# A two-layer encoder trunk on one core: tanh for silu beside the heads, scores in single banks, a one-tensor maxima step, and another order of the first fetches

## The chip, the cores and the metric

The kernel runs on one core of a Trainium2 chip. Its engines are TensorE (PE, with its weight loads PEld), VectorE (DVE), ScalarE (ACT), GpSimd (POOL) and SyncE (SP, which here only issues DMAs). They run side by side, each through its own list of instructions in order, and wait for each other by semaphores. The metric is the device time of one execution in microseconds (us), as the median of several runs.

## The reference

Two inputs, `x_sample` (512 tokens) and `x_prompt` (1024 tokens), pass through the same trunk of two layers with a width of 1024. All arithmetic is float32.

```python
def fourier_mixer(x, g, w):                       # layer 0
    h = rms_norm(x, g).reshape(b, s, 8, 128)
    return jnp.real(jnp.fft.fft2(h, axes=(1, 3), norm="ortho")).reshape(b, s, d) @ w

def attention_mixer(...):                         # layer 1: 8 query heads, 2 key heads of 128
    q, k, v = split(rms_norm(x, g) @ w_qkv)
    q, k = apply_rope(rms_norm(q)), apply_rope(rms_norm(k))
    p = softmax(q @ k.T * 128 ** -0.5)            # per head, float32
    return (p @ v) @ w_o

def swiglu_ffn(x, g, w_gate, w_up, w_down):       # after each mixer, inner width 2816
    h = rms_norm(x, g)
    return (jax.nn.silu(h @ w_gate) * (h @ w_up)) @ w_down

for i in range(2):
    x = x + (fourier_mixer if i == 0 else attention_mixer)(x, ...)
    x = x + swiglu_ffn(x, ...)
```

## The kernel before

Tokens are worked in three blocks of 512 (`TB`): block 0 is sample, blocks 1 and 2 are prompt. Activations lie transposed, 128 features by 512 tokens a tile. Each float32 product is three PE passes over operands that are split into a high part (a cast on ACT) and a low rest (a subtraction on DVE or POOL): `split` writes both (lines 242 and 243), `mm3` issues the three matmuls (lines 249 to 251). So every weight chunk costs a load, an ACT cast and a POOL subtraction before PE can use it.

The stages in order of time: the **front** (mixer of sample, with the Fourier transform as matmuls), sample's first SwiGLU woven with prompt's mixer, prompt's first SwiGLU (both blocks together, by a scheme with seven products for eight), then from about 1300 us the **heads**: sample's attention, and prompt's attention woven with sample's second SwiGLU; at the end prompt's second SwiGLU. Two generators are woven by `weave`: stage "F" is the main one, stage "X" the one beside it. Each `yield` gives an estimated cost, and the generator that is behind runs next. A scheduler then sets the final order of each engine's list; instructions through `pinned` keep the order in which they were written.

The front. `turned_weights` prepares the mixer's weight in eight pieces. `load(n)` fetches piece n (line 637, queue of SP), `operand(n)` forms the sum of its halves on DVE (line 648) and the difference on POOL (line 649), casts on ACT (line 651) and subtracts on POOL (line 652); `product(n)` multiplies it on PE (g, with line 667 for an odd row, and c at line 669) and stores it for prompt. `lead` weaves it with `mixer("s", ...)`, which needs sample's rows (`load_rows`, line 404, four pieces on the queues of SP and ACT), their squares, the reciprocal root `r_s`, and the transform matrix `mat_s` (line 1453, POOL's queue). `busy(36)` is a run of matmuls on ones ahead of the first real one. `mixer_projection` multiplies the two results.

The heads. In `attend`, `scores(qc)` makes the scores of 128 queries: for prompt against 1024 keys in one tile of two PSUM banks (`bank2`, one buffer), for sample against 512 keys in one bank (`bankg`). Then come the maxima on DVE (line 1371, one per bank), their maximum times the negative gain (line 1372, the *maxima step*), the exponential on ACT with its row sum (line 1375), the reciprocal on DVE (line 1376) and the scaling on ACT (line 1377). `turned` transposes the result on PE (line 1389) and splits it; `values` multiplies by v. `side` and `sides` give spare banks to other helpers of the same stage.

Sample's second SwiGLU is `ffn(1, 0, ...)`, where `here` is false: 22 chunks of the gate go through silu (line 852) on ACT, which stands in the same list as the exponentials:

```python
dve.tensor_tensor(ga, ga, first["r"], op=ALU.mult)
act.activation(s, ga, AF.Silu)
pool.tensor_tensor(s, s, first["r"], op=ALU.mult)
dve.tensor_tensor(up, up, s, op=ALU.mult)
```

Of the kernel before, what the change touches and what calls it, by code (L numbers as in the profile page):

```python
# [17 lines left out]
P = 128  # L18
# [107 lines left out]
def trunk_kernel(ctx: ExitStack, tc: tile.TileContext, t: dict):  # L126
# [18 lines left out]
    for name, kw in (("sbH", {}), ("sbF", {}), ("sbX", {}), ("psF", PS), ("psX", PS)):  # L145
# [5 lines left out]
    BUFS = {  # L151
# [4 lines left out]
    }  # L156
    uid = [0]
# [37 lines left out]
    def bankg():  # L195
        return tl("g", [TB], F32, "gF", pools["psF"])

    def side():

        return bankg() if cur[0] == "F" else bank2()[:, 0]  # L200

    def sides():
        if cur[0] == "F":
            return [bankg(), bankg()]
        a2 = bank2()
        return [a2[:, 0], a2[:, 1]]

# [45 lines left out]
    early = []  # L253
    nxt, first = {}, {}

    def pinned(ins):
# [373 lines left out]
    def turned_weights(w64, dd, odd, alt):  # L630


        raws = []

        def load(n):
            raw = tl("raw", [2, TB], F32, "rawX")
            sp.dma_start(raw.rearrange("p k n -> p (k n)"), t["wf"][n])
            raws.append(raw)

        load(0)  # L640
        load(1)
        yield
        ods, ready = [], []

        def operand(n):
            raw = raws.pop(0)
            f = tl("f", [2, TB], F32, "rawF")
            pinned(dve.tensor_tensor(f[:, 0], raw[:, 0], raw[:, 1], op=ALU.add))
            pool.tensor_tensor(f[:, 1], raw[:, 0], raw[:, 1], op=ALU.subtract)
            w = moving_w[n % 4]  # L650
            pinned(act.copy(w[:, 0], f))
            pool.tensor_tensor(w[:, 1], f, w[:, 0].bitcast(F32), op=ALU.subtract)
            if n + 2 < NC:
                load(n + 2)
            ready.append(w)

        def product(n):
            h, j = divmod(n, 4)
            if j == 0:
                ods.append(tl("c", [TB], F32, "cX", pools["psX"]))  # L660
            od, w = ods[h], ready.pop(0)
            wt = tl("w", [2, 2, TB], F32R, "wX" if h else "wF")
            for k in range(2):
                ps = bankg()
                mm3(ps, dd[:, 2 * k], dd[:, 2 * k + 1], w[:, 0, k], w[:, 1, k], True, k == 1)
                if k == 0:
                    pe.matmul(ps, alt[0:96, j], w64[0:96, h * TB : (h + 1) * TB], start=False, stop=True)
                    for b in range(2):
                        pe.matmul(od[0:96], odd[:, 8 - 2 * j : 104 - 2 * j], w[:, b, 0], start=j == 0 and b == 0, stop=j == 3 and b == 1)
                split(wt[:, 0, k], wt[:, 1, k], ps)  # L670
                c = tl("t", [TB], F32, "tX")
                act.copy(c, ps)
                sp.dma_start(cwd[h][:, :, k, j, :], c.rearrange("p (n c) -> p n c", n=4))
            turned.append(wt)
            if j == 3:
                stacked(odds[0:96, h * TB : (h + 1) * TB], od[0:96], 64)

        for n in range(3):
            operand(n)
            yield  # L680
        for n in range(NC):
# [77 lines left out]
    def ffn(layer, b, h, out=None):  # L759
# [50 lines left out]
        for fc in range(NF):  # L810
# [41 lines left out]
            act.activation(s, ga, AF.Silu)  # L852
            pool.tensor_tensor(s, s, first["r"], op=ALU.mult)
            dve.tensor_tensor(up, up, s, op=ALU.mult)
            m = tl("mid", [2, TB], F32R, "mid")
            split(m[:, 0], m[:, 1], up)
            if odd_:
# [13 lines left out]
    def moving(blocks, gain, out, ring, helped):  # L871
# [23 lines left out]
        for j in range(4):  # L895
            flush()
            x4, v = loaded.pop()
            a2 = bank2()
            for (d, k), x in list(v.items()):
                if d == k:  # L900
                    v[d, k] = a2[:, d]
# [423 lines left out]
    def attend(blocks, straight, slot):  # L1325
# [6 lines left out]
        for g in range(NKV):  # L1332
# [24 lines left out]
            for h in range(g * GROUP, (g + 1) * GROUP):  # L1357
# [2 lines left out]

                def scores(qc):
                    qs = slice(qc * P, (qc + 1) * P)
                    sc = bankg().unsqueeze(1) if nb == 1 else bank2()
                    for kb in range(nb):
                        ks = slice(kb * TB, (kb + 1) * TB)
                        mm3(sc[:, kb], qt[:, 0, qs], qt[:, 1, qs], kt[:, 0, ks], kt[:, 1, ks], True, True)
                    s_in = sc[:, 0:nb].rearrange("p b n -> p (b n)")
                    gq = 4 * blocks[0] + qc
                    st = col(3)
                    for kb in range(nb):  # L1370
                        dve.tensor_reduce(st[:, 2 * kb : 2 * kb + 1], sc[:, kb], op=ALU.max, axis=AX.X)  # L1371
                    dve.scalar_tensor_tensor(st[:, 1:2], st[:, 2 * nb - 2 : 2 * nb - 1], st[:, 0:1], nrqc[:, gq, h : h + 1], op0=ALU.max, op1=ALU.mult)  # L1372
                    sm = col(2)
                    p = tmp(T) if nb == 1 else tl("p", [T], F32, "pX", ap)
                    act.activation(p, s_in, AF.Exp, bias=st[:, 1:2], scale=rqc[:, gq, h : h + 1], accum_out=sm[:, 0:1])  # L1375
                    dve.reciprocal(sm[:, 1:2], sm[:, 0:1])
                    act.activation(p, p, AF.Copy, scale=sm[:, 1:2])
                    return p
# [63 lines left out]
    got_s, got_p = {}, {}  # L1442

    def row_in(seq):
        m = mpt.tile([P, 2, 258], F32R, tag="rowm", name=f"rowm_{seq}")
        pool.dma_start(m[0:1].rearrange("p h n -> p (h n)"), t[f"row_{seq}"])
        rows_m[seq] = m
# [7 lines left out]
    row_in("s")  # L1455
# [19 lines left out]
    ws = turned_weights(w64, dd, odd, alt)  # L1475

    def lead():
        next(ws)
        sp.dma_start(stage[0:96], t["wf64"])
        m = mixer("s", got_s, u_s, xrs_s, zz_s)  # L1480
        for k, v in enumerate(m):
            yield v
            if k == 3:
                stacked(w64[0:96], stage[0:96], 64)
            if k < 3 or k % 2 == 0 and k < 14:
                next(ws)

    def follow():
        m = mixer_projection("s", got_s)
        for k in range(3):  # L1490
            next(m)
            next(ws)
            yield 1.0
        for _ in ws:
            yield 1.0
# [30 lines left out]
    def aux_0():  # L1526
        load_rows("p")
        row_in("p")
        m_p = [acc_tile("mat_p", [2, 1028], F32R) for _ in range(2)]
        for c in range(2):  # L1530
            pool.dma_start(m_p[c].rearrange("p h n -> p (h n)"), t["dft_p"][:, 2056 * c : 2056 * (c + 1)])
# [177 lines left out]
```

## Time and profile before

| | us |
|---|---|
| median of 3 runs (2921.27 to 2924.79) | 2921.47 |
| the profiled execution: time | 2916.32 |
| the profiled execution: span | 2914.5 |
| PE busy | 2834.5 (97%) |
| ACT table loads, 26 of 1.283 us | 33.4 |

The span runs from the first to the last instruction. A busy PE is not PE at its peak, since matmuls are pipelined and a lowered clock makes them longer; the granted clock was 0.996 on average. In the groups, `out<-in` are tile names without buffer numbers, `x96` is a count, then follow the busy time and the mean in ns of one, and behind the bar the idle time of the engine before them and what ended it.

### The profile page before, as it was taken

What the parts mean: (1) busy time and instruction counts of PE and PEld (TensorE: products, weight loads), DVE (VectorE), ACT (ScalarE), POOL (GpSimd) and SP (SyncE); (2) the same over time, 40 slices, a digit from 0 to 9 for tenths busy, and PEclk for the clock granted to TensorE, in tenths of its full rate; (3) what the DMA queues carried; (4) which work ended last, traced back from release to release, by engine and by line L of the source; (5) the groups of instructions that cost most, each with busy time, mean ns of one, the idle gap of its engine ahead of it and who ended that gap; (6) DMA issues with size and microseconds to landing.
All of it is one profiled execution on the core that took longest, in us unless ns stands there. A gap on an engine that the chain in (4) does not pass through costs nothing.

```text
span 2914.5 us, 37209 instructions
## 1 busy us (share of the span) xinstructions
PE 2834.5 (97%) x13656; PEld 2341.5 (80%) x13656; DVE 1714.5 (59%) x3023; ACT 1304.7 (45%) x2134; POOL 1573.4 (54%) x976
## 2 busy tenths in 40 slices
PE   7999999999999999999999999999999999999999
PEld 6778878888888887787778888888888788888887
DVE  6664562466666666847656565553345466666666
ACT  6543242333333333646757776763333333333332
POOL 4445375767776676432332123224637667766774
PEclk9999999999999999999999999999999999999999
DMA  7435474766556653732332112115448865566553
GB/s 233 143 113 179 139 285 174 287 210 227 195 178 215 219 188 112 238 93 92 94 102 84 34 63 71 55 55 184 159 151 303 326 237 195 179 215 221 195 174 116
DMA packets 178870, 490.53 MB, mean 168 GB/s; under 512 B 19488, under 2 KB 29728, under 8 KB 177280
## 3 DMA queue, kind: packets, MB, share of 16 engines
q1 hardware_dynamic: 177760, 483.36, 48.7%
q0 software_dynamic: 640, 3.74, 0.4%
q8 instruction: 108, 1.77, 0.3%
q10 hardware_dynamic: 288, 1.05, 0.1%
q14 instruction: 74, 0.61, 0.1%
HBM read 422.01 MB, written 66.06 MB: 167 GB/s over the span
## 4 chain that ended last, share of the span: by engine, by line
PE 44%; DVE 3%; issue 2%; ACT 1%; DMA 1%; POOL 1%; SPq 0%; POOLq 0%; DVEq 0%; ACTq 0%
PE a L249 6%; PE a L251 6%; PE a L250 6%; PE c L249 5%; PE c L250 5%; PE c L251 5%; PE g L251 3%; PE g L249 3%; PE g L250 3%; PE c L1389 2%; DVE col L1372 1%; DVE col L1371 1%; DVE acc L1074 1%; POOL w L288 0%; ACT p L1375 0%
## 5 line engine op out<-in xcount | busy, mean ns | idle before, releaser
L288 POOL TENSOR_TENSOR w<-raw,w 128x1024 fp32r<-128x1024 f32 x200 | 479.6, 2404 | 762.3 <-ACT w L287 713.8
L243 POOL TENSOR_TENSOR w<-raw,w 128x512 fp32r<-128x512 f32 (+1 forms) x464 | 608.7, 1332 | 443.6 <-ACT w L242 431.6
L242 ACT CAST w<-raw 128x512 fp32r<-128x512 f32 (+1 forms) x464 | 279.5, 632 | 541.1 <-PE a L251 179.7
L287 ACT CAST w<-raw 128x1024 fp32r<-128x1024 f32 x200 | 209.4, 1049 | 275.2 <-PE g L251 94.5
L249 PE MATMUL g<-h,w 128*128 128x512 f32 x704 | 279.0, 396 | 3.5 <-DVE ss L339 2.0
L249 PE MATMUL a<-ring,w 128*128 128x512 f32 x708 | 277.4, 392 | 0.0
L251 PE MATMUL g<-h,w 128*128 128x512 f32 x704 | 276.2, 392 | 0.0
L250 PE MATMUL g<-h,w 128*128 128x512 f32 x704 | 276.1, 392 | 0.0
L251 PE MATMUL a<-ring,w 128*128 128x512 f32 x708 | 275.9, 390 | 0.0
L250 PE MATMUL a<-ring,w 128*128 128x512 f32 x708 | 275.7, 389 | 0.0
L1074 DVE TENSOR_TENSOR acc<-g,acc 128x512 f32<-128x512 f32 x294 | 201.8, 687 | 105.1 <-PE g L251 104.9
L1074 DVE TENSOR_TENSOR acc<-c,acc 128x512 f32<-128x512 f32 x294 | 201.7, 686 | 92.8 <-PE c L251 91.2
L249 PE MATMUL c<-mid,w 128*128 128x512 f32 x604 | 237.0, 392 | 7.0 <-DVE acc L780 4.9
L250 PE MATMUL c<-mid,w 128*128 128x512 f32 x604 | 236.4, 391 | 4.8 <-DVE mid L243 4.8
L251 PE MATMUL c<-mid,w 128*128 128x512 f32 x604 | 236.1, 391 | 0.0
L249 PE MATMUL c<-h,w 128*128 128x512 f32 x480 | 190.5, 398 | 2.1 <-ACT h L245 1.6
L250 PE MATMUL c<-h,w 128*128 128x512 f32 x480 | 188.7, 395 | 0.4 <-DVE h L246 0.2
L251 PE MATMUL c<-h,w 128*128 128x512 f32 x480 | 188.2, 393 | 0.0
L780 DVE TENSOR_TENSOR acc<-c,acc 128x512 f32<-128x512 f32 x176 | 121.0, 688 | 112.7 <-PE c L251 111.8
L249 PEld LDWEIGHTS a<-ring,w 128*128 128x128 f32 x708 | 133.0, 188 | 32.1 <-DVE mid L243 4.3
L249 PEld LDWEIGHTS g<-h,w 128*128 128x128 f32 x704 | 132.5, 188 | 30.1 <-DVE ss L339 2.2
L251 PEld LDWEIGHTS a<-ring,w 128*128 128x128 f32 x708 | 133.1, 188 | 27.9
(393 smaller groups left out, 6727.5 us busy)
## 6 DMA issues: line engine op xcount, KB each, us to landing
ring<-mov_B SPq DMA_DIRECT2D x248, 512.0 KB, 5.5
ring<-mov_T SPq DMA_DIRECT2D x88, 512.0 KB, 5.2
raw<-in_gate_dram SPq DMA_DIRECT2D x44, 512.0 KB, 3.6
raw<-in_up_dram SPq DMA_DIRECT2D x44, 512.0 KB, 3.5
raw<-in_down_dram SPq DMA_DIRECT2D x88, 256.0 KB, 3.0
raw<-in_gate_dram SPq DMA_DIRECT2D x88, 256.0 KB, 5.1
raw<-in_up_dram SPq DMA_DIRECT2D x88, 256.0 KB, 5.3
raw<-in_down_dram SPq DMA_DIRECT2D x44, 512.0 KB, 4.3
```

Of the source, the lines that this page charges most:

```text
L242: keep(act.copy(hi, src))
L243: keep(eng.tensor_tensor(lo, src, hi.bitcast(F32), op=ALU.subtract))
L249: pe.matmul(out, lh, rh, start=first, stop=False, **kw)
L250: pe.matmul(out, lh, rl, start=False, stop=False, **kw)
L251: pe.matmul(out, ll, rh, start=False, stop=last, **kw)
L287: pinned(act.copy(flat[:, 0], raw)) if early else act.copy(flat[:, 0], raw)
L288: pool.tensor_tensor(flat[:, 1], raw, flat[:, 0].bitcast(F32), op=ALU.subtract)
L780: dve.tensor_tensor(acc[dc], box[0], acc[dc], op=ALU.add)
L1074: dve.tensor_tensor(acc, chain[d], acc, op=ALU.add)
L1371: dve.tensor_reduce(st[:, 2 * kb : 2 * kb + 1], sc[:, kb], op=ALU.max, axis=AX.X)
L1372: dve.scalar_tensor_tensor(st[:, 1:2], st[:, 2 * nb - 2 : 2 * nb - 1], st[:, 0:1], nrqc[:, gq, h : h + 1], op0=ALU.max, op1=ALU.mult)
L1389: pe.transpose(tr[:, i * P : (i + 1) * P], p[:, kc * P : (kc + 1) * P], ident)
```

## The change

Four edits. In `ffn`, where `here` is false, silu(x) is computed as 0.5 x (1 + tanh(x/2)): a tanh on ACT, a new SCALAR_TENSOR_TENSOR on DVE, and the factor 0.5 in the last product. In the heads, once `apart` is set (just before prompt's attention), scores lie in two tiles of one bank each instead of one tile of two, with two buffers of that kind; the exponential is issued once per bank, and a small sum joins the two row sums. `side`, `sides` and `moving` take single banks from then on. The maxima step is a `tensor_scalar` with two per-partition scalars. In the front, piece 0 of the weight is fetched ahead of sample's rows, and `mask`, `mat_s` and the short row `rowm_s` are issued later, inside `lead`.

```diff
+    def single():
+        return tl("a", [TB], F32, "gH", pools["psX"])
     def side():
-        return bankg() if cur[0] == "F" else bank2()[:, 0]
+        return bankg() if cur[0] == "F" else single() if apart else bank2()[:, 0]
...
         load(0)
+        yield
         load(1)
         yield
...
-            act.activation(s, ga, AF.Silu)
+            if here:
+                act.activation(s, ga, AF.Silu)
+            else:
+                act.activation(s, ga, AF.Tanh, scale=0.5)
+                dve.scalar_tensor_tensor(s, s, 1.0, ga, op0=ALU.add, op1=ALU.mult)
             pool.tensor_tensor(s, s, first["r"], op=ALU.mult)
-            dve.tensor_tensor(up, up, s, op=ALU.mult)
+            if here:
+                dve.tensor_tensor(up, up, s, op=ALU.mult)
+            else:
+                dve.scalar_tensor_tensor(up, up, 0.5, s, op0=ALU.mult, op1=ALU.mult)
...
-                    sc = bankg().unsqueeze(1) if nb == 1 else bank2()
+                    sc = [bankg()] if nb == 1 else sides()
...
-                    dve.scalar_tensor_tensor(st[:, 1:2], st[:, 2 * nb - 2 : 2 * nb - 1], st[:, 0:1], nrqc[:, gq, h : h + 1], op0=ALU.max, op1=ALU.mult)
-                    sm = col(2)
+                    dve.tensor_scalar(st[:, 1:2], st[:, 2 * nb - 2 : 2 * nb - 1], st[:, 0:1], nrqc[:, gq, h : h + 1], op0=ALU.max, op1=ALU.mult)
+                    sm = col(3)
                     p = tmp(T) if nb == 1 else tl("p", [T], F32, "pX", ap)
-                    act.activation(p, s_in, AF.Exp, bias=st[:, 1:2], scale=rqc[:, gq, h : h + 1], accum_out=sm[:, 0:1])
+                    for kb in range(nb):
+                        act.activation(p[:, kb * TB : (kb + 1) * TB], sc[kb], AF.Exp, bias=st[:, 1:2], scale=rqc[:, gq, h : h + 1], accum_out=sm[:, 2 * kb : 2 * kb + 1])
+                    if nb == 2:
+                        dve.tensor_scalar(sm[:, 0:1], sm[:, 0:1], sm[:, 2:3], None, op0=ALU.add)
...
-    load_rows("s")
     m_s = acc_tile("mat_s", [2, 2, 514], F32R)
-    pool.dma_start(m_s.rearrange("p c h n -> p (c h n)"), t["dft_s"])
...
-    sp.dma_start(mask, t["mask"])
+    ws = turned_weights(w64, dd, odd, alt)
+    next(ws)
+    load_rows("s")
     zz_s = zeros("s")
...
     def lead():
         next(ws)
+        sp.dma_start(mask, t["mask"])
+        next(ws)
+        pool.dma_start(m_s.rearrange("p c h n -> p (c h n)"), t["dft_s"])
         sp.dma_start(stage[0:96], t["wf64"])
+        row_in("s")
+        rows_of_dft("s")
```

What the scheduler makes of it. In the front, POOL's list before began with the matrix `mat_s`, the short row and the constants (`eo`), and then came the first differences of the weight's pieces:

```order
L1453 DMA mat_s_162<-in_dft_s_dram 128x2056
masks.py:199 ISA
masks.py:199 AFFINE_SELECT ident<-ident 128x128
L1446 DMA rowm_s<-in_row_s_dram 1x12x43
L1460 DMA eo_166<-in_dft_d_dram 128x1136
L443 MEMSET t_172 128x480
L649 TENSOR_TENSOR f_266<-raw_239 128x512
L649 TENSOR_TENSOR f_283<-raw_241 128x512
L652 TENSOR_TENSOR wm_169<-f_266,wm_169 128x1024
```

The same place now (line numbers are those of the changed kernel, tile numbers differ):

```order
L1473 DMA eo_157<-in_dft_d_dram 128x1136
masks.py:199 ISA
masks.py:199 AFFINE_SELECT ident<-ident 128x128
L448 MEMSET t_170 128x480
L655 TENSOR_TENSOR f_240<-raw_162 128x512
L1494 DMA mat_s_156<-in_dft_s_dram 128x2056
L1463 DMA rowm_s<-in_row_s_dram 1x12x43
L655 TENSOR_TENSOR f_273<-raw_237 128x512
L658 TENSOR_TENSOR wm_160<-f_240,wm_160 128x1024
```

The constants come first, and the matrix and the short row are issued between the first two differences. PE's list in the front before, from the second half of piece 0 (g_345) on, where c_402 and c_414 are the mixer's:

```order
L251 MATMUL g_345<-wm_169,eo_166 128x512
L669 MATMUL c_331<-wm_169,eo_166 96x512 x4
L249 MATMUL c_402<-mat_s_162,comb_238 128x258
L250 MATMUL c_402<-mat_s_162,comb_238 128x258
L249 MATMUL c_414<-mat_s_162,comb_238 128x258
```

And now, from the same place to the first matmul that reads the matrix:

```order
L256 MATMUL g_327<-wm_160,eo_157 128x512
L675 MATMUL c_313<-wm_160,eo_157 96x512 x2
L673 MATMUL g_315<-eo_157 128x512
L675 MATMUL c_313<-wm_160,eo_157 96x512
L254 MATMUL g_362<-wm_160,eo_157 128x512
...
L673 MATMUL g_403<-eo_157 128x512
L254 MATMUL g_415<-wm_160,eo_157 128x512
L255 MATMUL g_415<-wm_160,eo_157 128x512
L256 MATMUL g_415<-wm_160,eo_157 128x512
L254 MATMUL c_431<-mat_s_156,comb_236 128x258
```

The products of pieces 0, 1 and 2 (g_315 to g_415) now stand ahead of the mixer. In the heads, DVE's list before, around the maxima step of one chunk of prompt's attention (pt is the split transposed result of the chunk before):

```order
L1371 TENSOR_REDUCE col_13746<-a_13739 128x1 x2
L243 TENSOR_TENSOR pt_13761<-c_13763,pt_13761 128x4x128
L1372 SCALAR_TENSOR_TENSOR col_13746<-col_13746,nrqc 128x1
L243 TENSOR_TENSOR pt_13762<-c_13770,pt_13762 128x4x128
L1376 RECIPROCAL col_13750<-col_13750 128x1
```

And now, with the tanh's new step (L862) between the maxima of two banks:

```order
L1383 TENSOR_REDUCE col_13870<-a_13862 128x1
L862 SCALAR_TENSOR_TENSOR t_13977<-t_13977,g_13712 128x512
L1383 TENSOR_REDUCE col_13870<-a_13863 128x1
L1384 TENSOR_SCALAR col_13870<-col_13870,nrqc 128x1
L1390 TENSOR_SCALAR col_13874<-col_13874 128x1
L1391 RECIPROCAL col_13874<-col_13874 128x1
```

The small sum L1390 is new and stands ahead of the reciprocal. ACT's list at a silu before:

```order
L852 ACT_TABLE_LOAD
L852 ACTIVATE t_14313<-g_13922 128x512
L242 CAST pt_14039<-c_14085 128x4x128
L242 CAST pt_14040<-c_14092 128x4x128
L1375 ACT_TABLE_LOAD
L1375 ACTIVATE p_14081,col_14080<-a_14069,col_14076,rqc 128x1024
```

And now at a tanh (L861), between the halves of a chunk's exponential and its scaling (L1392):

```order
L1388 ACTIVATE p_13599,col_13598<-a_13586,col_13594,rqc 128x512
L1388 ACTIVATE p_13599,col_13598<-a_13587,col_13594,rqc 128x512
L247 CAST pt_13560<-c_13612 128x4x128
L861 ACTIVATE t_13688<-g_13318 128x512
L1392 ACTIVATE p_13599<-p_13599,col_13598 128x1024
```

No table load stands there any more; the whole list has 4 where it had 26.

More of the change, by code (lines that the diff above doesn't have):

```diff
@@ L204, in sides @@
             return [bankg(), bankg()]
+        if apart:
+            return [single(), single()]
         a2 = bank2()
@@ L251, in mm3 @@
         pe.matmul(out, ll, rh, start=False, stop=last, **kw)
-    early = []
+    early, apart = [], []
     nxt, first = {}, {}
@@ L897, in moving @@
             x4, v = loaded.pop()
-            a2 = bank2()
+            a2 = sides()
             for (d, k), x in list(v.items()):
                 if d == k:
-                    v[d, k] = a2[:, d]
+                    v[d, k] = a2[d]
                 dve.scalar_tensor_tensor(v[d, k], x, gain[:, 4 * d + j : 4 * d + j + 1], r[k], op0=ALU.mult, op1=ALU.mult)
@@ L1362, in scores @@
                     qs = slice(qc * P, (qc + 1) * P)
-                    sc = bankg().unsqueeze(1) if nb == 1 else bank2()
+                    sc = [bankg()] if nb == 1 else sides()
                     for kb in range(nb):
                         ks = slice(kb * TB, (kb + 1) * TB)
-                        mm3(sc[:, kb], qt[:, 0, qs], qt[:, 1, qs], kt[:, 0, ks], kt[:, 1, ks], True, True)
-                    s_in = sc[:, 0:nb].rearrange("p b n -> p (b n)")
+                        mm3(sc[kb], qt[:, 0, qs], qt[:, 1, qs], kt[:, 0, ks], kt[:, 1, ks], True, True)
                     gq = 4 * blocks[0] + qc
@@ L1370, in scores @@
                     for kb in range(nb):
-                        dve.tensor_reduce(st[:, 2 * kb : 2 * kb + 1], sc[:, kb], op=ALU.max, axis=AX.X)
-                    dve.scalar_tensor_tensor(st[:, 1:2], st[:, 2 * nb - 2 : 2 * nb - 1], st[:, 0:1], nrqc[:, gq, h : h + 1], op0=ALU.max, op1=ALU.mult)
-                    sm = col(2)
+                        dve.tensor_reduce(st[:, 2 * kb : 2 * kb + 1], sc[kb], op=ALU.max, axis=AX.X)
+                    dve.tensor_scalar(st[:, 1:2], st[:, 2 * nb - 2 : 2 * nb - 1], st[:, 0:1], nrqc[:, gq, h : h + 1], op0=ALU.max, op1=ALU.mult)
+                    sm = col(3)
                     p = tmp(T) if nb == 1 else tl("p", [T], F32, "pX", ap)
-                    act.activation(p, s_in, AF.Exp, bias=st[:, 1:2], scale=rqc[:, gq, h : h + 1], accum_out=sm[:, 0:1])
+                    for kb in range(nb):
+                        act.activation(p[:, kb * TB : (kb + 1) * TB], sc[kb], AF.Exp, bias=st[:, 1:2], scale=rqc[:, gq, h : h + 1], accum_out=sm[:, 2 * kb : 2 * kb + 1])
+                    if nb == 2:
+                        dve.tensor_scalar(sm[:, 0:1], sm[:, 0:1], sm[:, 2:3], None, op0=ALU.add)
                     dve.reciprocal(sm[:, 1:2], sm[:, 0:1])
@@ L1444, in row_in, with rows_of_dft @@
     def row_in(seq):
-        m = mpt.tile([P, 2, 258], F32R, tag="rowm", name=f"rowm_{seq}")
-        pool.dma_start(m[0:1].rearrange("p h n -> p (h n)"), t[f"row_{seq}"])
-        rows_m[seq] = m
+        rows_m[seq] = mpt.tile([P, 2, 258], F32R, tag="rowm", name=f"rowm_{seq}")
+    def rows_of_dft(seq):
+        pool.dma_start(rows_m[seq][0:1].rearrange("p h n -> p (h n)"), t[f"row_{seq}"])
     turned = []
     odds = mpt.tile([P, D], F32R, name="odds")
-    load_rows("s")
     m_s = acc_tile("mat_s", [2, 2, 514], F32R)
-    pool.dma_start(m_s.rearrange("p c h n -> p (c h n)"), t["dft_s"])
     mats["s"] = [m_s[:, 0], m_s[:, 1]]
-    row_in("s")
     slot = h_slot("eo", F32R, "B")
@@ L1482, in lead @@
             yield v
-            if k == 3:
+            if k == 1:
                 stacked(w64[0:96], stage[0:96], 64)
-            if k < 3 or k % 2 == 0 and k < 14:
+            if k < 2 or k % 2 == 0 and k < 14:
                 next(ws)
@@ L1491, in follow @@
             next(m)
-            next(ws)
+            next(ws, None)
             yield 1.0
@@ L1528, in aux_0 @@
         row_in("p")
+        rows_of_dft("p")
         m_p = [acc_tile("mat_p", [2, 1028], F32R) for _ in range(2)]
@@ L1609, in trunk_kernel @@
     open_pool("psX", **RIGHT, **PS)
+    apart.append(True)
     ap = open_pool("ap", **RIGHT)
```

1 line of the change is left out of this document (removed), and 2 rows, old and new, of the table BUFS.

## The prediction

> **What bounds the kernel now.** I read first the page's busy line, then a table of stages, then who waits for whom inside the two stages that the change touches.
>
> ```profile
> PE 2834.5 (97%) x13656; PEld 2341.5 (80%) x13656; DVE 1714.5 (59%) x3023; ACT 1304.7 (45%) x2134; POOL 1573.4 (54%) x976
> core 0: us, PE busy (x) PEld busy (x) DVE busy (x) ACT busy (x) POOL busy (x), PEclk, DMA share, GB/s
> 0.00:20.00 20.00, 14.80 (x89) 13.60 (x89) 9.47 (x17) 10.12 (x19) 7.73 (x13) 1.00 0.82 287
> 20.00:30.00 10.00, 3.70 (x10) 1.74 (x10) 9.35 (x23) 4.61 (x7) 7.54 (x5) 0.83 0.36 111
> 30.00:40.00 10.00, 6.37 (x18) 4.69 (x19) 7.62 (x11) 6.02 (x12) 3.21 (x3) 0.50 0.62 208
> 40.00:100.00 60.00, 53.69 (x346) 46.69 (x345) 44.27 (x101) 38.70 (x69) 25.65 (x16) 1.00 0.64 196
> 100.00:1300.00 1200.00, 1183.82 (x5491) 973.88 (x5490) 713.91 (x1231) 462.65 (x769) 725.67 (x451) 1.00 0.56 191
> 1300.00:2000.00 700.00, 669.58 (x3743) 560.47 (x3742) 414.06 (x839) 470.36 (x730) 203.97 (x97) 1.00 0.24 77
> 2000.00:2300.00 300.00, 294.86 (x1307) 243.21 (x1306) 113.23 (x188) 96.60 (x144) 173.67 (x98) 0.99 0.64 219
> ```
>
> TensorE (PE) bounds the program and no matmul is added or removed, so all that can be won is time in which PE stands still or runs at a lowered clock. PE is idle for 2914.5 - 2834.5 = 80.0 us. Two stages hold most of it: the front (0 to 100 us), 100 - 14.80 - 3.70 - 6.37 - 53.69 = 21.4 us, and the heads (1300 to 2000 us), 700 - 669.58 = 30.4 us. PE works through one list in order, so a gap that closes there moves everything behind it; from 2000 us on PE is nearly full and the saving arrives at the end.
>
> **The heads: what PE waits for.** The view of waits, PE alone, 1300 to 2000 us (total, times, longest), then the maxima step L1372 in the view of one line (min/median/max ns, and who waited), the by-form groups on VectorE (DVE), and one piece of the timeline.
>
> ```profile
> PE a L249 <- ACT p L1375: 7.2, 7, 2.1
> PE c L1389 <- ACT p L1377: 5.0, 5, 1.5
> PE c L1389 <- DVE h L243: 3.4, 4, 1.4
> PE c L1389 <- ACT t L1403: 2.1, 2, 1.3
> PE c L1389 <- ACT t L1377: 1.4, 1, 1.4
> PE g L249 <- ACT t L1375: 1.3, 2, 0.9
> L1372 DVE SCALAR_TENSOR_TENSOR col<-col,nrqc x96: 199/218/2407, 1342.3 to 1976.3; 128x1 f32<-128x1 f32 x96
>   ACT p L1375: 49.2, 35
> L1372 DVE SCALAR_TENSOR_TENSOR col<-col,nrqc 128x1 f32<-128x1 f32 x96 | 59.6, 624 | 1.1
> L1376 DVE RECIPROCAL col<-col 128x1 f32<-128x1 f32 x96 | 15.4, 160 | 51.8 <-ACT p L1375 43.9 <-ACT t L1375 7.5
> 1576.42 2.41 POOL L243 TENSOR_TENSOR w<-raw,w 128x1024 fp32r<-128x1024 f32 x1 [6.37 <-ACT w L242]
> 1576.58 2.27 DVE L1372 SCALAR_TENSOR_TENSOR col<-col,nrqc 128x1 f32<-128x1 f32 x1
> 28.13 2.60 POOL L652 TENSOR_TENSOR wm<-f,wm 128x1024 fp32r<-128x1024 f32 x1
> 28.45 0.13 DVE L437 TENSOR_SCALAR m<-m 128x1 f32<-128x1 f32 x1
> ```
>
> L1372 handles one element a partition, yet its mean is 624 ns against a median of 218. The timeline shows why: it starts 0.16 us after a GpSimd (POOL) instruction and ends with it (1578.85 against 1578.83). It reads two tensors from SBUF. L1376 reads one, is as small, and stays at 160 ns on average over 96 instructions. The exponential (L1375, ScalarE, ACT) waits for L1372 for 49.2 us in all, the scores' bank is free only after the exponential, and PE's transposes (L1389) need its scaled result.
>
> **Part 1, the maxima step with one tensor (96 instructions).** The two maxima and the gain become one tensor and two per-partition scalars of a TENSOR_SCALAR. The nearest row of that form is L437: 0.13 us in the middle of a POOL instruction that runs from 28.13 to 30.73. If the new step behaves so, it costs some 0.2 us, the old median, and 96 x (0.624 - 0.218) = 39 us of blocked DVE time go. What of it lies on PE's path is at most the six waits above, which all stand behind the softmax chain or behind DVE's queue: 7.2 + 5.0 + 3.4 + 2.1 + 1.4 + 1.3 = 20.4 us. A lower bound is 0 (the new form waits as the old). I take 17, because the blockings (up to 2.4 us) are as long as PE's gaps (up to 2.1 us); the rest has other causes.
>
> The Trainium skill, "SBUF — State Buffer", section "Who interferes with whom", says that a VectorE instruction with two SBUF inputs contends with a GpSimd instruction that reads SBUF, and the second to issue waits for the whole of the first; the trace agrees (2.27 us beside 2.41). The same section lists tensor_scalar among the operations that can take both ports and then contend; by that the saving would be 0. The section "What auto-detection actually checks" of the Trainium skill's "VectorE: DVE Perf Modes" speaks of the outermost non-unit dimensions of source and destination for that mode, and a column of one element has none; the 0.13 us of L437 agrees.
>
> **Part 2, silu by tanh in sample's second SwiGLU, and part 3, exponentials by halves.** Table loads, and the shapes that the halves are priced by:
>
> ```profile
> L1375 ACT ACT_TABLE_LOAD x12 | 15.4, 1283 | 0.2
> L852 ACT ACT_TABLE_LOAD x12 | 15.4, 1283 | 0.2
> L1375 ACT ACTIVATE p<-a,col,rqc 128x1024 f32<-128x1024 f32 x64 | 77.4, 1209 | 49.5 <-DVE col L1372 49.2
> L1375 ACT ACTIVATION_READ_ACCUMULATOR p<-a,col,rqc 128x1 f32 x64 | 12.3, 192 | 0.0
> L1375 ACT ACTIVATE t<-g,col,rqc 128x512 f32<-128x512 f32 x32 | 24.9, 779 | 17.2 <-DVE col L1372 17.2
> L1307 DVE SCALAR_TENSOR_TENSOR t<-c,gains,rope 128x512 f32<-128x512 f32 x13 | 9.7, 748 | 11.2 <-ACT a L1306 10.9 <-issue 0.3
> 1619.21 1.28 ACT L852 ACT_TABLE_LOAD   x1
> 1619.24 0.50 PE L249 MATMUL a<-w,w 128*128 128x512 f32 x1 [2.11 <-ACT p L1375]
> ```
>
> In the new program 22 of the table loads are gone: 22 x 1.283 = 28.2 us of ACT. The tanh itself I price as the silu. DVE gets 22 more SCALAR_TENSOR_TENSOR of 128x512 (748 ns by L1307): 16.5 us. The halves turn 64 x (1.209 + 0.192) into 64 x 2 x (0.779 + 0.192), +34.6 us of ACT, and add 64 small sums on DVE (0.16 us each by L1376, 10 us). Net: ACT +6.4 us on 470 in a stage of 700, DVE 16.5 + 10 - 39 = -12.5 us on 414. Both engines stay under 70% busy, which covers the work as such. Not covered is the chain of one chunk of 128 queries: exponential to scaled result grows by 0.54 + 0.16 = 0.7 us. PE's list puts other matmuls between a chunk's scores and its transposes; where that cover runs out a wait of up to 0.7 us appears. Bounds: 0, and 64 x 0.7 = 45 us. The blockings that go are worth more per chunk (mean 0.4 us, up to 2.2) and only short gaps were there, so I take +2, near the low end.
>
> The two single banks give back: the first bank is free after the first half, some 1.209 - 0.779 = 0.43 us sooner. For the 7 waits on L1375 that is 3 us, which overlap with part 1; a table load stands beside a PE wait only now and then (1619.24 is one, and that wait is for the exponential before the load). I take 2 for banks and 1 for table loads. Heads in sum: -17 - 2 - 1 + 2 = -18 us; bounds +45 (every chunk waits, nothing gained) and -30.4 (all of the stage's idle time).
>
> The Trainium skill, "ScalarE: Activation LUTs", section "What ACT_TABLE_LOAD costs", counts a drain of 1380 ns beside each load, 2.66 us a switch: by that 22 loads would free 58.5 us of ACT. This trace does not show it (idle 0.2 us before twelve loads).
>
> **Part 4, the front.** Weights' first piece is fetched before sample's rows, the transform matrix goes behind POOL's first sum, the constants for the weights move ahead of it.
>
> ```profile
> 8.67 1.29 DVE L424 TENSOR_TENSOR x<-c,x 128x512 f32<-128x512 f32 x2 [7.67 <-DMA x<-in_rows_s_dram]
> 11.98 0.69 DVE L424 TENSOR_TENSOR x<-c,x 128x512 f32<-128x512 f32 x1 [2.03 <-DMA x<-in_rows_s_dram]
> 14.59 1.28 POOL L649 TENSOR_TENSOR f<-raw 128x512 f32<-128x512 f32 x1 [10.67 <-DMA raw<-in_wf_dram]
> 19.08 0.47 PE L249 MATMUL g<-wm,eo 128*128 128x512 f32 x1
> PE c L669 <- POOL wm L652: 4.7, 3, 2.0
> PE c L669 <- ACT wm L651: 3.0, 3, 1.6
> 39.14 2.37 POOL L652 TENSOR_TENSOR wm<-f,wm 128x1024 fp32r<-128x1024 f32 x1 [6.72 <-ACT wm L651]
> ```
>
> The first piece takes the place in SP's queue that the first rows had, so POOL can start near 8.7 instead of 14.59, and the rows' two SP pieces slip one place each, about 3.3 us (11.98 - 8.67). The warm-up matmuls keep PE until about 19, so the first weight product starts no sooner; but products 0 to 3 then find operands ready instead of waiting. On POOL the matrix's issue and the short row's now stand behind a sum that waits for a landing, and POOL's second sum stands behind them. The matrix's first consumers stand behind three weight products in PE's new list (before, behind one), so I cost this at nothing; that cover gone, it would be the 3.3 us again. To be had: PE idle from 20 to 40 us, 6.30 + 3.63 = 9.9 us, and the low clock (0.83 and 0.50: 3.70 x 0.17 + 6.37 x 0.50 = 3.8 us), 13.7 together. Against it, DVE is 9.35 and 7.62 of 10 busy there and the mixer starts 3.3 us later. Bounds: -13.7 and +3.3. I take half of the upper one, -7, since ACT has room from 20 to 40 (4.61 and 6.02) but DVE has little.
>
> **Sum.** -18 - 7 = -25 us. Against the profiled execution (span 2914.5, time 2916.32) that is a span of 2889.5; the median of the three runs shown lies 5.15 us above the profiled execution, and my time is for such a median: 2921.47 - 25 = 2896.5.
>
> **Rivals.** (a) The maxima step still waits for POOL. For it: of the same operation, TENSOR_SCALAR, one of three at 128x32 (L1323) took 2.39 us:
>
> ```profile
> L1323 DVE TENSOR_SCALAR nrqc<-col x3: 174/175/2392, 1336.9 to 1527.1; 128x32 f32<-128x32 f32 x3
> ```
>
> Against: L437 at 128x1. Then the heads keep their gaps and win 1 for banks and tables less costs: -7 - 1 = 2913.5. (b) The front wins nothing since DVE and the later rows take over as its limit: 2903.5. (c) Slower: ACT's longer chain (0.7 us a chunk) is not covered, and PE waits for each chunk's scaled result. At the full 45 us instead of my 2 that is 2896.5 + 43 = 2939.5; it decides from (25 + 2) / 64 = 0.42 us of new waiting per chunk. For it: ACT is already the busiest helper (470 of 700). Against: PE waited for L1377 only 5 times. (d) Neither part reaches PE, because its other waits move up: 2921.
>
> **How the numbers follow.** Forecast 0.60, (a) 0.13, (b) 0.17, (c) 0.06, (d) 0.04. The time is the forecast's, 2896.5. The range, 2884 to 2914, takes in (a) and (b), and below, heads at -24 with the front at its bound of -13.7; (c) and (d) and the far ends stay out. A measurement of this kernel can tell about 0.2%, 5.8 us, from no change. Faster by more: 0.60 + 0.17 + most of (a) = 0.87; within: part of (a) and (d), 0.07; slower: (c), 0.06.
>
> **What will show it.** Right: the maxima step's maximum near 0.25 us whatever POOL does; PE idle in the heads under 15 us; four table loads in all; PE idle from 20 to 40 us under 5 us, and the front's later work some 7 us earlier. Wrong: the step's maximum still above 2 us; PE's transposes waiting for the scaled result more than ten times; PE's first products waiting for the matrix or the rows.

## The result and the profile after

The changed kernel takes 2899.15 us (median of 4 runs, 2897.86 to 2899.62), the kernel before 2921.37 us beside it (2918.89 to 2924.79). The ratio is 0.9922 with an interval of 0.9910 to 0.9935: faster by 22.2 us, where 25 were forecast. The sum came out nearly right, but two of its terms were wrong, and a cost that was in no term hides between them.

First the busy line of the changed kernel's page.

```profile
PE 2842.4 (98%) x13656; PEld 2347.0 (81%) x13656; DVE 1723.1 (59%) x3109; ACT 1295.3 (45%) x2240; POOL 1574.0 (54%) x976
```

Its stages, with the columns of the table before:

```profile
20.00:30.00 10.00, 6.16 (x16) 4.14 (x17) 9.87 (x14) 4.35 (x7) 7.94 (x4) 0.77 0.42 125
30.00:40.00 10.00, 7.15 (x19) 4.45 (x17) 9.44 (x22) 7.84 (x13) 6.70 (x4) 0.55 0.73 203
1300.00:2000.00 700.00, 688.15 (x3836) 580.55 (x3835) 414.54 (x928) 468.30 (x845) 213.37 (x100) 1.00 0.26 82
2000.00:2300.00 300.00, 298.53 (x1319) 244.38 (x1318) 128.69 (x214) 101.08 (x154) 183.91 (x107) 1.00 0.67 235
```

PE's idle time in the heads fell from 30.4 to 700 - 688.15 = 11.85 us, and from 2000 to 2300 us from 5.1 to 1.5 us. But the span is 2897.0, so all idle time is 2897.0 - 2842.4 = 54.6 us, 25.4 less than the 80.0 before, while the span shrank by only 17.5. The rest is in the first number of the page: PE is busy 7.9 us *longer* (2842.4 against 2834.5) with the same 13656 matmuls. Idle time alone doesn't show where that went; the experiments do.

The maxima step in the view of one line (min/median/max ns):

```profile
L1384 DVE TENSOR_SCALAR col<-col,nrqc x96: 254/273/276, 1346.0 to 1960.0; 128x1 f32<-128x1 f32 x96
```

One instance in the timeline, beside GpSimd's row (start, duration in us):

```profile
1429.21 2.41 POOL L293 TENSOR_TENSOR w<-raw,w 128x1024 fp32r<-128x1024 f32 x1 [1.70 <-ACT w L292]
1429.42 0.27 DVE L1384 TENSOR_SCALAR col<-col,nrqc 128x1 f32<-128x1 f32 x1
```

What PE waits for from 1300 to 2000 us, the three longest and the wait for the scaled result (total, times, longest):

```profile
PE c L322 <- ACT t L1308: 2.5, 1, 2.5
PE g L256 <- POOL w L248: 2.0, 3, 1.3
PE a L254 <- ACT p L1388: 1.7, 1, 1.7
...
PE c L1404 <- ACT p L1392: 0.5, 1, 0.5
```

The step's maximum over all 96 is 276 ns, against 2407 before, and the one at 1429.42 us ends long before the GpSimd instruction around it does. The six softmax waits that summed to 20.4 us have shrunk to single ones; the wait for the exponential is 1.7 us once instead of 7.2 us in seven times, the wait for the scaled result 0.5 us once instead of 5.0 us in five.

The front, in the view of one tile each: the reciprocal root `r_s`, and `rs`, the last one of the front (first and last start in us). Before:

```profile
L302 DVE SCALAR_TENSOR_TENSOR r_s<-c,col x1: 161/161/161, 25.4 to 25.4; 128x4 f32<-128x4 f32 x1
L302 DVE SCALAR_TENSOR_TENSOR rs<-c,col x1: 161/161/161, 98.7 to 98.7; 128x4 f32<-128x4 f32 x1
```

After:

```profile
L307 DVE SCALAR_TENSOR_TENSOR r_s<-c,col x1: 150/150/150, 32.6 to 32.6; 128x4 f32<-128x4 f32 x1
L307 DVE SCALAR_TENSOR_TENSOR rs<-c,col x1: 161/161/161, 98.5 to 98.5; 128x4 f32<-128x4 f32 x1
```

A wait of PE that was not there before, from 0 to 100 us after:

```profile
PE c L675 <- DVE x L432: 2.8, 1, 2.8
```

The mixer's tiles y and the product's c take turns in the same two PSUM buffers, so this product had to wait until VectorE had finished the step L432 on the rows. The first products do come earlier, but the root comes 7.2 us later and the front ends where it ended.

### The profile page after: what moved, and what is told of

It is laid out like the page before. It is cut to its first block, busy times and chain, and to the rows that moved or that the text cites. A ratio compares the mean times of both kernels' runs of the same rounds, so it can differ in the third digit from the quotient of the medians.

```text
span 2897.0 us, 37468 instructions
## 1 busy us (share of the span) xinstructions
PE 2842.4 (98%) x13656; PEld 2347.0 (81%) x13656; DVE 1723.1 (59%) x3109; ACT 1295.3 (45%) x2240; POOL 1574.0 (54%) x976
## 4 chain that ended last, share of the span: by engine, by line
PE 84%; DVE 5%; DMA 3%; ACT 3%; issue 3%; POOL 2%; SPq 0%; ACTq 0%; DVEq 0%; POOLq 0%
PE a L254 11%; PE a L256 11%; PE a L255 11%; PE c L254 9%; PE c L255 9%; PE c L256 9%; PE g L254 6%; PE g L256 6%; PE g L255 6%; PE c L1404 2%; POOL w L293 1%; DMA raw<-in_up_dram 1%; DVE acc L1087 1%; ACT w L292 1%; PE c L1272 1%
## 5 line engine op out<-in xcount | busy, mean ns | idle before, releaser
L248 POOL TENSOR_TENSOR w<-raw,w 128x512 fp32r<-128x512 f32 (+1 forms) x464 | 608.6, 1332 | 428.1 <-ACT w L247 405.0
L254 PE MATMUL c<-h,w 128*128 128x512 f32 x480 | 192.4, 402 | 2.1 <-ACT h L250 1.6
L255 PE MATMUL c<-h,w 128*128 128x512 f32 x480 | 190.6, 398 | 0.2
L256 PE MATMUL c<-h,w 128*128 128x512 f32 x480 | 190.4, 398 | 0.0
L254 PEld LDWEIGHTS g<-h,w 128*128 128x128 f32 x704 | 132.9, 189 | 30.4 <-DVE ss L344 2.0
```

Source lines behind the costliest of these rows:

```text
L248: keep(eng.tensor_tensor(lo, src, hi.bitcast(F32), op=ALU.subtract))
L254: pe.matmul(out, lh, rh, start=first, stop=False, **kw)
```

## The experiments

The times of the kernel before beside these runs were 2919.44, 2918.53 and 2919.0 us in three sets (runs one to four, the next four, the last four). A ratio is formed within its set; where two runs of different sets are compared and it changes the reading, the difference of their ratios, times 2919 us, is given beside that of their medians.

**The maxima step alone, and all but it.** First the kernel before with this edit alone, then the changed kernel with this edit taken back.

```diff
-dve.scalar_tensor_tensor(st[:, 1:2], st[:, 2 * nb - 2 : 2 * nb - 1], st[:, 0:1], nrqc[:, gq, h : h + 1], op0=ALU.max, op1=ALU.mult)
+dve.tensor_scalar(st[:, 1:2], st[:, 2 * nb - 2 : 2 * nb - 1], st[:, 0:1], nrqc[:, gq, h : h + 1], op0=ALU.max, op1=ALU.mult)
```

> The kernel before with the maxima step alone as a one-tensor TENSOR_SCALAR. Theory A (the step's wait for POOL is what PE's gaps in the heads stand on): 14 to 18 us faster than before, step at 0.27 us throughout, PE idle from 1300 to 2000 us falls from 30 to under 17 us. Rival B (single banks and half exponentials carry the gain): under 5 us faster. Rival C (the 22 table loads carry it): under 5 us faster.

> The changed kernel with only the maxima step put back to two tensors. Theory A: the step is again up to 2.4 us long and most of the gain is gone, 4 to 8 us faster than before at the most. Rivals B and C: still 17 to 22 us faster than before.

Alone it gives 2895.53 us, ratio 0.9913 (0.9899 to 0.9927): 24 us, more than the whole change. Without it the other edits together give 2915.26 us, 0.9986 (0.9977 to 0.9994), 4 us. The step's line and the heads where it is alone:

```profile
L1372 DVE TENSOR_SCALAR col<-col,nrqc x96: 256/266/275, 1347.2 to 1958.0; 128x1 f32<-128x1 f32 x96
```

```profile
1300.00:2000.00 700.00, 690.20 (x3856) 582.66 (x3855) 386.24 (x854) 478.43 (x740) 215.22 (x102) 1.00 0.26 83
```

And the line where it is left out:

```profile
L1384 DVE SCALAR_TENSOR_TENSOR col<-col,nrqc x96: 193/220/2396, 1344.7 to 1974.1; 128x1 f32<-128x1 f32 x96
```

So the wait for GpSimd carries most of the gain, and the rivals that put all of it on single banks or on table loads fall. What the other edits are worth can't be read from the 4 us: this run differs from the kernel before in one more thing, which the paragraph on placement finds. That the part gives more than the whole was not explained here either.

**The front.** The changed kernel with the front of before, and the kernel before with the new front alone (a part of the second edit; the first is its reverse).

```diff
-    load_rows("s")
...
-    pool.dma_start(m_s.rearrange("p c h n -> p (c h n)"), t["dft_s"])
...
+    ws = turned_weights(w64, dd, odd, alt)
+    next(ws)
+    load_rows("s")
```

> The changed kernel with the front (order of the first fetches) of the kernel before. Theory D (the front's new order wins nothing, since DVE is full there and the rows come later): 22 to 27 us faster than before, thus 0 to 4 us faster than the changed kernel. Rival E (the front's order is worth the 7 us of my prediction and something else took them back): 15 us faster than before, 7 us slower than the changed kernel.

> The kernel before with the new order of the front alone. Theory D: between 1 us faster and 4 us slower than before; the first block of sample's SwiGLU starts as late as before or 1 to 3 us later. Rival E: 5 to 8 us faster.

2898.51 us, 0.9927 (0.9915 to 0.9940), and 2920.09 us, 1.0002 (0.9994 to 1.0010). The new front is worth nothing that can be measured, alone or in company. To see what holds it, the third run left the sums and differences of the eight weight pieces out, and with them a part of the mixer's arithmetic:

```diff
-            f = tl("f", [2, TB], F32, "rawF")
-            pinned(dve.tensor_tensor(f[:, 0], raw[:, 0], raw[:, 1], op=ALU.add))
-            pool.tensor_tensor(f[:, 1], raw[:, 0], raw[:, 1], op=ALU.subtract)
+            f = raw
```

> The changed kernel, whose eight pieces of the front's weight skip the sum on VectorE and the difference on GpSimd: the raw halves are cast and subtracted instead (this leaves out a part of the mixer's arithmetic). Fetches and their order stay. Theory D1 (VectorE, full and blocked by GpSimd, sets the front's pace): without 8 sums of 0.7 us, the time they wait for GpSimd and that in which they block others, the reciprocal root comes 4 us sooner or more (32.6 us in the changed kernel), the front ends at 94 or before (98.5), and the time falls by 4 us or more, to 2895 or less. Theory D2 (the rows that land later set it): the reciprocal root stays within 1.5 us of 32.6, and the time within 2 us of 2899.

It took 2893.29 us, 0.9912 (0.9899 to 0.9926), 5.9 less than the changed kernel; by the ratios it is 3 us, and the intervals overlap. Its two roots:

```profile
L307 DVE SCALAR_TENSOR_TENSOR r_s<-c,col x1: 161/161/161, 28.4 to 28.4; 128x4 f32<-128x4 f32 x1
L307 DVE SCALAR_TENSOR_TENSOR rs<-c,col x1: 161/161/161, 93.4 to 93.4; 128x4 f32<-128x4 f32 x1
```

Both come earlier by what the theory of a full VectorE asked for (4.2 and 5.1 us). Four runs have the new front with its sums, and their roots lie at 32.0 to 32.6 and at 97.9 to 98.5 us, so this is more than their spread. The changed kernel's timeline shows the same thing: the sum L654 waits for GpSimd, and other work stands ahead of the root.

```profile
11.48 1.89 DVE L429 TENSOR_TENSOR x<-c,x 128x512 f32<-128x512 f32 x3 [1.72 <-DMA x<-in_rows_s_dram]
16.88 2.21 DVE L654 TENSOR_TENSOR f<-raw 128x512 f32<-128x512 f32 x1
22.70 1.79 DVE L633 TENSOR_TENSOR eo<-stage,eo 32x1024 fp32r<-32x1024 f32 x1
25.13 1.06 DVE L654 TENSOR_TENSOR f<-raw 128x512 f32<-128x512 f32 x1
27.41 2.38 POOL L658 TENSOR_TENSOR wm<-f,wm 128x1024 fp32r<-128x1024 f32 x1 [1.76 <-ACT wm L657]
27.68 2.65 DVE L654 TENSOR_TENSOR f<-raw 128x512 f32<-128x512 f32 x1
31.98 0.69 DVE L248 TENSOR_TENSOR w<-g,w 128x512 fp32r<-128x512 f32 x1 [0.16 <-ACT w L247]
```

VectorE is busy 9.87 and 9.44 of 10 us from 20 to 40 us, part of it blocked: the sum takes 2.65 us at 27.68, since it reads two SBUF tensors while GpSimd works from 27.41 to 29.79. The rows that land later are little of the root's 7.2 us: VectorE starts on them at 11.48 us, and from there to the root it is idle once, for 0.16 us. Before, it had done 1.29 us of that work when the third piece came at 11.98 us, so the later rows cost under 1 us. The way from there to the root took 13.5 us before (11.98 to 25.44) and takes 21.1 us now (11.48 to 32.59), because three sums of 5.92 us in all stand in it instead of two of 2.07 us, L633 with 1.79 us, and two more subtractions L248. The run without sums also frees the fetched pieces sooner and unloads GpSimd; how much of the 5 us is each was not separated.

**What kind of TENSOR_SCALAR stays clear of GpSimd.** The changed kernel with the front of before, prompt's 64 steps two columns wide (shortened: the maxima now go to columns 2 and 3, and sample's steps keep the narrow form):

```diff
-dve.tensor_scalar(st[:, 1:2], st[:, 2 * nb - 2 : 2 * nb - 1], st[:, 0:1], nrqc[:, gq, h : h + 1], op0=ALU.max, op1=ALU.mult)
+dve.tensor_scalar(st[:, 4:6], st[:, 2:4], st[:, 2:3], nrqc[:, gq, h : h + 1], op0=ALU.max, op1=ALU.mult)   # where nb == 2
```

> The changed kernel with the front of before, and the 64 maxima steps of prompt's chunks made two columns wide (TENSOR_SCALAR 128x2, still one tensor and two per-partition scalars); the 32 steps of sample stay 128x1. Its counterpart is the changed kernel with the front of before: 2898.5 us. Width theory: it is the single column that keeps the step from waiting for POOL (a TENSOR_SCALAR of 128x32 took up to 2392 ns). Then the 64 wide steps reach up to 2.4 us again, with a mean near 0.5 us, and two thirds of the 17 us between that kernel and the changed kernel with two tensors come back: some 2909 us. Tensor-count theory: it is the number of tensors read that decides, and the 128x32 had another cause. Then the wide steps stay near 0.28 us at most and the time at 2898.

2900.73 us, 0.9938 (0.9925 to 0.9952). The wide steps and sample's narrow ones in the same run:

```profile
L1387 DVE TENSOR_SCALAR col<-col,nrqc x64: 276/289/2407, 1524.2 to 1962.4; 128x2 f32<-128x2 f32 x64
L1384 DVE TENSOR_SCALAR col<-col,nrqc x32: 255/272/276, 1340.1 to 1473.7; 128x1 f32<-128x1 f32 x32
```

An instance in its timeline, and its heads:

```profile
1533.17 2.40 POOL L293 TENSOR_TENSOR w<-raw,w 128x1024 fp32r<-128x1024 f32 x1 [6.25 <-ACT w L292]
1534.17 1.43 DVE L1387 TENSOR_SCALAR col<-col,nrqc 128x2 f32<-128x2 f32 x1
```

```profile
1300.00:2000.00 700.00, 679.49 (x3799) 571.45 (x3798) 423.71 (x912) 466.09 (x842) 211.06 (x100) 1.00 0.25 80
```

The block is back: one tensor of two columns waits until GpSimd ends (1534.17 + 1.43 = 1535.60, against 1533.17 + 2.40 = 1535.57), and PE is idle for 20.5 us in the heads again. So here it is the single column that escapes, not the single tensor. Yet the time is only 2 us above its counterpart instead of 11. That is the second thing that did not add up.

**Tanh, and single banks, each beside the maxima step.** The edits are shown in part; the kernel before is what they change.

```diff
-            act.activation(s, ga, AF.Silu)
...
+                act.activation(s, ga, AF.Tanh, scale=0.5)
+                dve.scalar_tensor_tensor(s, s, 1.0, ga, op0=ALU.add, op1=ALU.mult)
```

> The kernel before with two of the four edits: the one-tensor maxima step, and silu by tanh. With the maxima step alone it was 2895.5 us. Theory 1 (tanh costs: 22 more VectorE instructions of about 0.75 us, 16.5 us, stand in the list that also makes the maxima, and their two SBUF inputs wait for POOL): 2897 to 2900. Theory 2 (tanh wins: 22 table loads of 1.283 us less on ScalarE, some of them in front of an exponential): 2890 to 2894. Rival (neither reaches TensorE): 2895.5 within 1.5.

```diff
-                    sc = bankg().unsqueeze(1) if nb == 1 else bank2()
+                    sc = [bankg()] if nb == 1 else sides()
...
-                    sm = col(2)
+                    sm = col(3)
```

> The kernel before with two other edits: the one-tensor maxima step, and scores in two single banks with exponentials by halves. With the maxima step alone it was 2895.5 us. Theory 1 (the longer chain on ScalarE costs: 64 chunks with one more instruction, 0.44 us longer each, partly uncovered): 2897 to 2902. Theory 2 (banks that come free 0.4 us sooner win): 2892 to 2894. Rival (hidden): 2895.5 within 1.5. If neither this nor the run with tanh differs from 2895.5, the 3 us between the maxima step alone and the whole change are the spread between program builds.

Tanh: 2886.69 us, 0.9894 (0.9878 to 0.9909), better than any forecast for it, though its interval still overlaps the one of the maxima step alone. Banks: 2900.09 us, 0.9934 (0.9922 to 0.9946). By the expectation that would be ScalarE's longer chain. But PE's idle time from 1300 to 2000 us grew by only 1.6 us (690.20 - 688.62), and a place where the heads play no part says otherwise. Here is the stretch from 600 to 1100 us, in prompt's first SwiGLU. Before, and one group by form in it:

```profile
600.00:1100.00 500.00, 500.00 (x2197) 410.61 (x2196) 324.06 (x499) 180.03 (x323) 361.16 (x255) 1.00 0.59 201
```

```profile
L251 PE MATMUL a<-op,w 128*128 128x512 f32 x72 | 28.0, 389 | 0.0
```

The same two of the changed kernel:

```profile
600.00:1100.00 500.00, 500.00 (x2188) 409.04 (x2187) 323.30 (x496) 178.13 (x319) 358.31 (x251) 1.00 0.60 203
```

```profile
L256 PE MATMUL a<-op,w 128*128 128x512 f32 x72 | 28.4, 394 | 0.0
```

The stretch with the maxima step alone:

```profile
600.00:1100.00 500.00, 500.00 (x2197) 410.68 (x2196) 325.26 (x500) 180.18 (x323) 360.93 (x254) 1.00 0.60 201
```

And with the maxima step and banks:

```profile
600.00:1100.00 500.00, 500.00 (x2188) 409.07 (x2187) 320.84 (x494) 178.05 (x319) 355.58 (x251) 1.00 0.60 203
```

PE is busy all 500 us at a granted clock of 1.00 in all four, and yet two of them get 9 matmuls less done, 0.4%. The two slower have one thing in common: `sm = col(3)`. The helper `col(n)` keeps four small buffers for each width. Once nothing asks for a width of 2, those buffers are gone, and most SBUF tiles allocated after them lie 128 bytes lower in each partition (a buffer of `mid`, the products that PE reads in the SwiGLUs: byte 109920 instead of 110048). Tiles that are allocated from the other end, `op` among them, stay. The two-column run, whose new `col(6)` takes the same 128 bytes, has x2197.

**Placement.** Four runs move addresses and no work. In the first three pairs the scheduler also puts a few hundred of PE's matmuls in another order, all of them behind 1300 us; in the fourth every engine's list stays the same in every place. The changed kernel with the width of 2 still in use:

```diff
-                    sm = col(3)
+                    sm = col(2) if nb == 1 else col(3)
```

> The changed kernel, in which sample's chunks keep the two-column tile for their sums: that tile's tag was gone with the change, and with it every later SBUF tile of that side lay 128 bytes lower (the middle products at byte 109920 of a partition, not 110048). Placement theory (matmuls run slower by some ns each in the builds with the lower addresses, whatever the stage: 2188 matmuls from 600 to 1100 us where the kernel before has 2197, that is 0.4% of a span of some 2300 us, 9 us): the count is 2197 again, the mean of a<-op,w is 389 ns and not 392 to 394, and the time is 2899.2 - 9 = 2890. Rival (the pace comes from the longer program or from the chip's state): 2188 and 2899.

The maxima step alone with `sm = col(3)`:

> The kernel before with the one-tensor maxima step (2895.5 us alone) and the tile for the sums three columns wide instead of two, nothing else: no instruction changes, only the addresses, which lie 128 bytes lower as in the changed kernel. Placement theory: 2188 matmuls from 600 to 1100 us and 2895.5 + 9 = 2904.5. Rival (the pace belongs to the change's longer list): 2197 and 2895.5.

The maxima step and banks, with the edit of the first:

> The maxima step with single banks and exponentials by halves (2900.1 us), with the addresses of the kernel before put back by the two-column tile. Placement theory: 2900.1 - 9 = 2891, so that single banks win some 4 us over the maxima step alone (2895.5). Rival (the longer chain on ScalarE is what costs): 2898 to 2901.

The maxima step and tanh, with an unused tile `cp.tile([P, 32], F32)` ahead of the rest:

> The maxima step with tanh (2886.7 us, the fastest so far), with an unused tile of 128 bytes a partition ahead of the others, so that the addresses lie 128 bytes higher than before. If the pace depends on the address modulo 256 bytes: as slow as 128 bytes lower, 2188 matmuls and 2886.7 + 9 = 2895.5. If only the lower place is bad: 2197 and 2886.7.

| edits | addresses as before | 128 bytes off | difference |
|---|---|---|---|
| whole change | 2887.97 (0.9893) | 2899.15 (0.9922) | 11.2 |
| maxima step | 2895.53 (0.9913) | 2903.39 (0.9944) | 7.9 |
| maxima step, banks | 2889.91 (0.9896) | 2900.09 (0.9934) | 10.2 |
| maxima step, tanh | 2886.69 (0.9894) | 2896.36, higher (0.9922) | 9.7 |

All four came out as the placement theory said, within 2.1 us. The two runs of a pair come from different sets; by the ratios the differences are 8.5, 9.0, 11.1 and 8.2 us. In the second pair, whose text differs by the width alone, the intervals are apart (0.9899 to 0.9927 against 0.9931 to 0.9956); in the fourth they touch (0.9878 to 0.9909 against 0.9909 to 0.9934). The busy line and the stretch from 600 to 1100 us of the first run:

```profile
PE 2832.1 (98%) x13656; PEld 2345.2 (81%) x13656; DVE 1719.7 (60%) x3109; ACT 1295.4 (45%) x2240; POOL 1573.2 (55%) x976
```

```profile
600.00:1100.00 500.00, 500.00 (x2198) 410.69 (x2196) 323.90 (x499) 180.96 (x325) 360.38 (x253) 1.00 0.60 202
```

The stretch of the second, and of the fourth:

```profile
600.00:1100.00 500.00, 500.00 (x2188) 409.06 (x2187) 322.92 (x496) 178.98 (x322) 359.31 (x252) 1.00 0.60 202
```

```profile
600.00:1100.00 500.00, 500.00 (x2187) 409.03 (x2187) 322.58 (x496) 178.95 (x321) 359.60 (x253) 1.00 0.60 201
```

With the old addresses PE is busy 10.3 us less for the same matmuls (2842.4 - 2832.1), nearly all by which the medians differ (11.2). The other kernels fall in line: all seven with the old addresses have 2197 or 2198 matmuls from 600 to 1100 us, all seven with moved ones 2187 or 2188. So the hidden cost is settled: 8 to 11 us, for 128 bytes either way. Not every matmul pays it. In the fourth pair, from 600 to 1100 us, first the old addresses, then the moved ones:

```profile
L251 PE MATMUL a<-op,w 128*128 128x512 f32 x72 | 28.0, 389 | 0.0
L251 PE MATMUL a<-ring,w 128*128 128x512 f32 x273 | 106.3, 389 | 0.0
```

```profile
L252 PE MATMUL a<-op,w 128*128 128x512 f32 x72 | 28.4, 394 | 0.0
L252 PE MATMUL a<-ring,w 128*128 128x512 f32 x271 | 105.6, 390 | 0.0
```

For a<-op,w the tile `w` moves and `op` doesn't; for a<-ring,w both move alike. What about the addresses does it (which tiles have to stand how to each other) stays open; 128 bytes lower and 128 higher are equally slow.

It also mends three readings left over. The run without the maxima step has the lower addresses too (2188 matmuls), and they hid what the other edits win. PE's idle time in the whole span shows it. The busy lines of that run (span 2911.1) and of the step alone (span 2894.6):

```profile
PE 2845.9 (98%) x13656; PEld 2345.7 (81%) x13656; DVE 1739.3 (60%) x3109; ACT 1294.6 (44%) x2240; POOL 1572.8 (54%) x976
```

```profile
PE 2837.4 (98%) x13656; PEld 2348.9 (81%) x13656; DVE 1687.1 (58%) x3023; ACT 1304.5 (45%) x2134; POOL 1571.2 (54%) x976
```

PE is idle for 80.0 us before, for 2911.1 - 2845.9 = 65.2 us without the step, for 2894.6 - 2837.4 = 57.2 us with the step alone and for 54.6 us with all edits. With the placement cost taken off, the other edits alone would give not 4 us but an estimated 12 to 15 (4 + 8 to 4 + 11).

The two-column run has the good addresses, so its counterpart is 2887.97 (the new front, in that one, was worth 0): its 64 blocked steps cost 12.8 us, near the 11 expected, and not 2. And banks win 2895.53 - 2889.91 = 5.6 us rather than cost 4.6 (3.3 us at the moved addresses, 2903.39 - 2900.09), though the intervals of both comparisons overlap (0.9882 to 0.9909 against 0.9899 to 0.9927, and 0.9922 to 0.9946 against 0.9931 to 0.9956).

## Why the prediction was right, point by point

- **Maxima step, -17 (bounds 0 and -20.4): right in mechanism, too small.** It measured -24 alone (the two profiled executions differ by 2914.5 - 2894.6 = 19.9 us). The step itself takes 273 ns, not the 0.2 us assumed. PE's idle time in the heads fell by 690.20 - 669.58 = 20.6 us: all that the waits listed came to, not most of it, and what the median has beyond that was not located. Taken back from the whole change, at equal addresses, it costs 2915.26 - 2899.15 = 16 us (19 by the ratios): the other edits and the step win part of the same waits.
- **Banks -2, table loads -1, longer chain +2: too small, as far as shown.** Beside the maxima step, at equal addresses, tanh measures -8.8 at the old addresses (5.5 by the ratios) and -7.0 at the moved ones (2896.36 - 2903.39), banks with halves -5.6 and -3.3, all with overlapping intervals. What tanh wins by isn't shown: PE's idle time fell by 0.8 us in the first pair of profiles and by 5.2 us in the second. The two together with the new front add only 7.6 (2895.53 - 2887.97), so they too seem to share waits. Rival (c), the uncovered chain of ScalarE, did not happen: PE's transposes waited for the scaled result once. The four table loads came as counted (22 gone).
- **Front, -7: wrong.** The step that failed is "I take half of the upper one". It was taken because ScalarE had room; the run without the sums points to VectorE, of which the prediction said that it had little. It filled up, partly with sums blocked by GpSimd, and its work between rows and root grew from 13.5 to 21.1 us, which moved the root from 25.4 to 32.6 us. The mixer's later start, charged with 3.3 us as a bound, was under 1 us of that. Rival (b) forecast a front that wins nothing, and so it came; of the two limits that it named, VectorE held and the later rows hardly counted.
- **Not in the sum: +10 for placement.** The line `sm = col(3)` had no term: the sums were priced by VectorE's time alone. Its real cost was in PE's pace, also where the edits change nothing. At the old addresses the whole change measures 2919.0 - 2887.97 = 31 us, so heads of -31 and a front of 0, and then 8 to 11 us were lost again. That 25 forecast and 22 measured agree is luck: misses of opposite sign cancelled.
- **What was to show it**: the step's maximum (0.276 us), the heads' idle time (11.85 us, under 15) and four table loads stand. PE idle from 20 to 40 us is 3.84 + 2.85 = 6.7 us, not under 5, at a clock still of 0.77 and 0.55, and the front's later work is not 7 us earlier. PE's first products also wait once for the rows (2.8 us at L675), one of the three signs of being wrong, and it marks the wrong term.

On the two rules weighed: the Trainium skill, "SBUF — State Buffer", section "Who interferes with whom", says that a tensor_scalar can take both ports, when its operands meet the conditions for that, and then contends with GpSimd. The two-column step agrees (2407 ns at most); the one-column step never waited (276 ns at most). The Trainium skill's "VectorE: DVE Perf Modes", section "What auto-detection actually checks", makes the mode hang on the outermost non-unit dimensions of source and destination. The border between 128x1 and 128x2 agrees with that.

## What to carry to other kernels

A tiny VectorE instruction on a chain that everything waits for should be written so that GpSimd can't hold it: here one tensor of one column and two per-partition scalars, 0.27 us in all 96 cases instead of up to 2.4. When PE's busy time changes though its matmuls have not, compare how many matmuls start in a stage that the change doesn't touch: a difference there is none of the edit's work, and the addresses of the tiles are the first suspect, since any change of a buffer's size or number moves them. Before fetches are moved, look for the stage's full engine: here VectorE was full, and earlier fetches for the others gained nothing.

## What the runs showed of the hardware

- 128 bytes in the addresses of SBUF tiles made matmuls of the same shape, clock and operands slower, by 3 to 5 ns of 389 in one group (a<-op,w), by at most 1 ns in another (a<-ring,w), and by 0.4% in a stage where PE never waits: 8 to 11 us over the program, in four pairs of kernels.
- A TENSOR_SCALAR of 128x1 with two per-partition scalars took 254 to 276 ns in all 96 cases, one of them inside a GpSimd instruction of 2.41 us; one of 128x2 took up to 2407 ns.
- The front of before varies by almost as much as this change was to win there: with the same lists up to that point, `rs` came at 98.7 us before, at 98.8 us in the two-column run and at 103.31 us in the run with the front of before, at granted clocks from 40 to 100 us of 1.00, 0.96 and 0.90. The two runs of banks without tanh have it at 103.6 and 104.3 us; whether that is chance stays open. Differences of a few us there need medians, not two traces.
